# A recurrent (HGRN2) layer: the low parts of the projection weights are formed by VectorE in place of GpSimd

## The chip, the cores and the metric

One core of a Trainium2 chip. The metric is the device time of one execution in microseconds (us), the median of several runs.

## The reference

A backbone of two layers over 1024 latent tokens and 256 context tokens, width 1024: a bidirectional gated linear recurrence (HGRN2), then multi-head latent attention (MLA). Each layer normalises its input, scales and shifts it by vectors made from a conditioning vector (adaLN), mixes the tokens, projects back and adds a gated, normalised residual. The change lies in the first layer. What it computes, cut to its core:

```python
q, i_in, f_fw, f_bw, z = jnp.split(h @ w_in, 5, axis=-1)     # 16 heads of 128 each
for d, g in enumerate((f_fw, f_bw)):
    f = lb[d] + (1 - lb[d]) * sigmoid(g);  k = (1 - lb[d]) * sigmoid(-g)
# per head and direction, v = i_in, q = silu(q):
S_t = diag(f_t) S_{t-1} + k_t v_t^T;   o_t = S_t^T q_t
o = o_forward + o_backward
y = (rmsnorm(o, gain) * silu(z)) @ w_out
```

All of it is in float32. The kernel keeps that precision in the projections by writing each factor as a rounded high part and the rest, the low part, and adding three products.

## The kernel before, in words

**Matrices in two parts.** `split` makes the parts: ScalarE casts the source to the rounded type (line 214, `hi`), then an engine subtracts (line 215, `lo = src - hi`); without `eng` that engine is VectorE. `load_split` loads a piece of 128x1024 float32 (512 KB) into a `raw` tile by a DMA from SyncE's queue (line 286) and splits it into `wh` and `wl`. `wpool` has four buffers each for `wh` and `wl` and two for `raw`; the small adaLN products of line 125, which VectorE makes beside the recurrence, use the `raw` buffers too. `mm3` multiplies: three matmuls (lines 263 to 265), high by high, high by low, low by high.

**The layer.** `hgrn` runs over 16 heads. The 10 token tiles of 128 tokens (two of context, eight of latent) stand in groups of four, four and two. For a head it takes three weight tiles (`load_qfb`: q and the two forget gates), and for every group multiplies them (`feed`, PSUM tiles `g`), makes the gates and the keys (`gates`), and then in `levels` the products within a tile, in seven levels of a binary tree. A level has one product on TensorE (`products`, line 335, PSUM tiles `lv`, two banks, which are shared with `g`), whose result is put into `A` by VectorE (line 351, `copy_predicated`) or ScalarE, and VectorE and ScalarE make the operands `KX` and `QX` of the next level from those of this one (lines 384 to 386, 398). So a level's product waits for VectorE's work of the level before, and TensorE is given projection products of the next group, of the values or of the gate `z` in between. On every even head `values` projects the values of two heads (two weight tiles). Then come the projection of `z` (one weight tile, lines 540 to 548), the states between tiles (`states`, and `recur`, line 446), and the readout, whose rsqrt runs on GpSimd (lines 80 and 81).

**The order.** Nothing here is ordered by hand: a scheduler orders every engine's instructions by its own estimate of when each can start. Each engine then runs its list in that order, so an instruction that waits holds up all that stand behind it on its engine. GpSimd's list in this layer holds the subtractions of `wl` and the rsqrt work, and nothing else.

**The names.** `wl` and `wh` are the parts of a weight tile, `lv` a level product, `KX` and `QX` its operands, `QY` and `K` the other halves that are kept for later levels, `A` the products that are put together, `Ta` and `Tb` the decays of a level, `kd` and `q` the operands of the diagonal.

Of the kernel before, what the change touches and what calls it, by code (L numbers as in the profile page):

```python
# [18 lines left out]
P = 128  # L19
# [21 lines left out]
class Net:  # L41
# [12 lines left out]
    def t(self, pool, shape, dt, tag, **kw):  # L54
        self.uid += 1
        return pool.tile(shape, dt, tag=tag, name=f"{tag}_{self.uid}", **kw)
# [425 lines left out]

    def load_qfb(self, wpool, h):
        return [
            self.load_split(wpool, self.a["w_qfbz"][h, :, m], [P, self.KT, P], "w", eng=self.nc.gpsimd)
            for m in range(3)
        ]

# [5 lines left out]
    def values(self, pool, wpool, pp, hh, hl, h):  # L494
        nc, t, KT = self.nc, self.t, self.KT
        w = min(2, self.NH - h)
        kh = max(1, KT // 2)
        wv = [
            self.load_split(wpool, self.a["w_v"][h // 2, :, k : k + kh, : w * P], [P, kh, w * P], "w", eng=nc.gpsimd)
            for k in range(0, KT, kh)  # L500
        ]
        V2 = t(pool, [P, self.NT, 2, P], F32, "V")
        for c in range(0, self.NT, 2):
            m = min(2, self.NT - c)
            ps = t(pp, [P, 2, 2, P], F32, "g")
            for j in range(m):
                sl = slice((c + j) * P, (c + j + 1) * P)
                for k in range(KT):
                    wh, wl = (x[:, k % kh] for x in wv[k // kh])
                    self.mm3(ps[:, j, :w], hh[:, k, sl], hl[:, k, sl], wh, wl, k == 0, k == KT - 1)  # L510
            nc.scalar.copy(V2[:, c : c + m, :w], ps[:, :m, :w])
        return V2

    def hgrn(self, pool, wpool, pp, hh, hl, yT, wq0, ps0, side, late):
        nc, t, KT, a = self.nc, self.t, self.KT, self.a
        for h in range(self.NH):
            wq = wq0 if h == 0 else self.load_qfb(wpool, h)
            sts = []
            for c0, n in self.groups:
                G = n * P  # L520
                sl = slice(c0 * P, c0 * P + G)
                st = {}
                for m in range(3):
                    if h == 0 and ps0 and m < len(ps0[0]):
                        ps = ps0[0][m]
                    else:
                        ps = t(pp, [P, 512], F32, "g")[:, :G]
                        for k in range(KT):
                            self.feed([ps], wq[m : m + 1], (c0, n), hh, hl, k)
                    self.gates(h, m, ps, G, st, pool)  # L530
                if h == 0 and (c0, n) == self.groups[min(1, len(self.groups) - 1)]:
                    late()
                if h == 0 and ps0:
                    ps0.pop(0)
                self.levels(pool, pp, st, G)
                sts.append(st)
            if h % 2 == 0:
                V2 = self.values(pool, wpool, pp, hh, hl, h)
            V = V2[:, :, h % 2]
            wz = self.load_split(wpool, a["w_qfbz"][h, :, 3], [P, KT, P], "w", eng=nc.gpsimd)  # L540
            Z = t(pool, [P, self.NT * P], F32, "Z")
            for c0, n in self.groups:
                sl = slice(c0 * P, (c0 + n) * P)
                ps = t(pp, [P, 512], F32, "g")[:, : n * P]
                for k in range(KT):
                    self.feed([ps], [wz], (c0, n), hh, hl, k)
                nc.scalar.activation(Z[:, sl], ps, AF.Sigmoid)
                nc.vector.tensor_tensor(Z[:, sl], Z[:, sl], ps, ALU.mult)
            US = t(pool, [P, 2, self.NT, P], F32, "US")
            for g, st in zip(self.groups, sts):  # L550
                self.states(pool, pp, st, g, V, US)
            prev = self.recur(sts, US)
            for g, st in zip(self.groups, sts):
                self.readout(h, pool, pp, st, g, V, Z, US, prev, yT)
            side(h)
# [811 lines left out]
```

## Time and profile before

| | |
|---|---|
| median of 3 runs | 3215.31 us (3214.12 to 3218.83) |
| the profiled execution, its own time | 3215.2 us |
| its span, first to last instruction | 3213.4 us |
| mean granted TensorE clock | 0.995 of full speed |
| busy: TensorE, VectorE, ScalarE, GpSimd | 3155.7, 2092.5, 1685.5, 437.1 us |

The recurrent layer goes from about 70 to 1670 us of the span; the output projection, MLA and its output projection follow. Busy shares are means over stages with different limits; what a change in one stage is worth is read from that stage's stretch, from what TensorE waits for there.

### The profile page before, as it was taken

To read this page: it belongs to the slowest core of one execution; us is meant where nothing else is said; L and a number is where in the kernel's file an instruction comes from. 1 tells how busy PE (TensorE), PEld (TensorE's weight loads), DVE (VectorE), ACT (ScalarE), POOL (GpSimd) and SP (SyncE) were. 2 spreads that over 40 slices of the span, in tenths; PEclk is the share of its full clock that TensorE was granted. 3 is DMA by queue.
4 is the path that set the end of the run, shared out by engine and by line. 5 is a ranking of instruction groups with operands and counts; after the bars stand their busy time and mean duration, and the time that the engine had idled before them with its cause. 6 is when DMAs were issued, how large, how long until landed. Compare 5 with 4: busy or idle time off the path is not lost.

```text
span 3213.4 us, 52381 instructions
## 1 busy us (share of the span) xinstructions
PE 3155.7 (98%) x19860; PEld 2827.5 (88%) x19860; DVE 2092.5 (65%) x4680; ACT 1685.5 (52%) x4215; POOL 437.1 (14%) x424
## 2 busy tenths in 40 slices
PE   8899999999999999999999999999999999999999
PEld 7888989889898898898998878888999999999887
DVE  7676577666774767737566464535777777777742
ACT  6455455554554545545455565314666666666532
POOL 2111111111111121111100212210000000000000
PEclk8999999999999999999999999999999999999999
DMA  5110211102111120100115662331100010101261
GB/s 209 40 55 22 73 35 48 55 29 79 36 42 55 35 73 29 35 29 27 36 35 172 233 227 86 115 125 53 39 32 30 27 37 29 37 21 37 75 214 59
DMA packets 100012, 218.94 MB, mean 68 GB/s; under 512 B 10288, under 2 KB 47408, under 8 KB 99760
## 3 DMA queue, kind: packets, MB, share of 16 engines
q1 hardware_dynamic: 99760, 215.59, 20.3%
q8 instruction: 157, 2.57, 0.3%
q14 instruction: 95, 0.78, 0.1%
HBM read 175.70 MB, written 39.85 MB: 67 GB/s over the span
## 4 chain that ended last, share of the span: by engine, by line
PE 80%; DVE 11%; issue 4%; ACT 2%; DMA 2%; POOL 1%; SPq 0%; DVEq 0%; POOLq 0%; ACTq 0%
PE g L264 9%; PE g L265 9%; PE g L263 9%; PE lv L335 6%; PE pt L878 4%; PE o L464 3%; PE s L831 2%; PE pv L263 2%; PE pv L264 2%; PE pv L265 2%; PE s L832 2%; PE s L834 2%; PE s L835 2%; PE s L833 2%; PE lv L263 2%
## 5 line engine op out<-in xcount | busy, mean ns | idle before, releaser
L263 PE MATMUL g<-hh,wh 128*128 128x512 f32 (+1 forms) x1512 | 547.5, 362 | 0.3 <-DVE hh L253 0.2
L264 PE MATMUL g<-hh,wl 128*128 128x512 f32 (+1 forms) x1512 | 544.9, 360 | 0.0
L265 PE MATMUL g<-hl,wh 128*128 128x512 f32 (+1 forms) x1512 | 544.6, 361 | 0.0
L263 PEld LDWEIGHTS g<-hh,wh 128*128 128x128 f32 x1512 | 286.9, 190 | 37.1 <-DVE hh L253 0.4
L264 PEld LDWEIGHTS g<-hh,wl 128*128 128x128 f32 x1512 | 286.9, 190 | 35.4
L265 PEld LDWEIGHTS g<-hl,wh 128*128 128x128 f32 x1512 | 286.0, 189 | 35.4
L215 POOL TENSOR_TENSOR wl<-raw,wh 128x1024 fp32r<-128x1024 f32 x77 | 195.3, 2541 | 872.0 <-ACT wh L214 864.4
L335 PE MATMUL lv<-QX,KX 128*128 128x128 f32 x1920 | 268.5, 278 | 28.5 <-DVE KX L384 12.9
L837 DVE TENSOR_REDUCE mx<-s 128x1 f32<-128x512 f32 (+1 forms) x384 | 229.6, 598 | 96.1 <-PE s L835 95.1
L847 ACT ACTIVATE pr<-s,nm 128x512 f32<-128x512 f32 (+1 forms) x384 | 232.7, 614 | 101.4 <-DVE nm L843 95.1
L335 PEld LDWEIGHTS lv<-QX,KX 128*128 128x128 f32 x1920 | 245.8, 192 | 44.2 <-issue 16.4
L214 ACT CAST wh<-raw 128x1024 fp32r<-128x1024 f32 (+1 forms) x170 | 178.2, 1052 | 131.4 <-PE lv L264 38.9
L214 ACT CAST ph<-pt 128x512 fp32r<-128x512 f32 x320 | 187.7, 587 | 95.0 <-PE pt L878 85.3
L215 DVE TENSOR_TENSOR pl<-pt,ph 128x512 fp32r<-128x512 f32 x320 | 219.2, 686 | 12.5 <-ACT ph L214 12.4
L385 ACT COPY KX<-K 128x256 f32<-128x256 f32 (+1 forms) x288 | 109.2, 379 | 171.3 <-DVE K L386 127.5
L263 PE MATMUL g<-wh,hh 128*128 128x256 f32 (+2 forms) x676 | 197.4, 293 | 0.0
L263 PE MATMUL pv<-ph,vh 128*128 128x256 f32 x640 | 196.6, 307 | 0.0
L265 PE MATMUL g<-wl,hh 128*128 128x256 f32 (+2 forms) x676 | 196.3, 291 | 0.0
L878 PE MATMUL pt<-ident,pr 128*128 128x128 f32 x1280 | 191.8, 272 | 0.1
L264 PE MATMUL g<-wh,hl 128*128 128x256 f32 (+1 forms) x654 | 188.6, 288 | 0.0
L215 DVE TENSOR_TENSOR wl<-raw,wh 128x1024 fp32r<-128x1024 f32 x93 | 117.0, 1263 | 106.5 <-ACT wh L214 105.6
L265 PE MATMUL pv<-pl,vh 128*128 128x256 f32 x640 | 180.0, 281 | 0.0
(552 smaller groups left out, 8129.0 us busy)
## 6 DMA issues: line engine op xcount, KB each, us to landing
raw<-in_w_o SPq DMA_DIRECT2D x64, 512.0 KB, 3.9
raw<-in_w_qfbz SPq DMA_DIRECT2D x61, 512.0 KB, 3.8
raw<-in_ada_wT SPq DMA_DIRECT2D x32, 512.0 KB, 3.5
raw<-in_w_mo SPq DMA_DIRECT2D x24, 512.0 KB, 3.7
raw<-in_w_v SPq DMA_DIRECT2D x16, 512.0 KB, 3.6
yT<-Z SPq DMA_DIRECT2D x32, 256.0 KB, 2.0
raw<-in_w_z SPq DMA_DIRECT2D x16, 512.0 KB, 3.9
pyr<-yT SPq DMA_DIRECT2D x64, 128.0 KB, 3.7
```

The lines of the kernel that those rows point to most:

```text
L214: nc.scalar.copy(hi, src)
L215: (eng or nc.vector).tensor_tensor(lo, src, v32(hi), ALU.subtract)
L263: mm(ps, lh, rh, start=first, stop=False)
L264: mm(ps, ll, rh, start=False, stop=False)
L265: mm(ps, lh, rl, start=False, stop=last)
L335: nc.tensor.matmul(ps[:, sl], lhs[:, sl], rhs[:, sl], start=True, stop=True)
L385: cp(m12(N[:]), m12(Y))
L464: nc.tensor.matmul(o[:, sl], l, r, start=i == 0, stop=i == len(ops) - 1)
L831: mm(s[:, :w], qah[:, js], st["kh"][:, ks], start=True, stop=False)
L837: nc.vector.tensor_reduce(mx[:, b : b + 1], s[:, :w], AX.X, ALU.min)
L847: nc.scalar.activation(pr[:, o : o + w], sc[b][:, :w], AF.Exp, bias=nm, scale=-1.0, accum_out=sm[:, b : b + 1],)
L878: nc.tensor.transpose(tp[:, c, j * P : (j + 1) * P], prs[i][:, k * P : (k + 1) * P], self.ident)
```

## The change

All weight tiles of `hgrn` but the first three, which are loaded at the start by another function, had GpSimd as the engine of the subtraction. The change leaves the argument out, so that VectorE does it. There are 77 such tiles: three for each of 15 heads, 16 of `values` and 16 of `z`. Shapes, buffers, DMAs and casts stay.

```diff
     def load_qfb(self, wpool, h):
         return [
-            self.load_split(wpool, self.a["w_qfbz"][h, :, m], [P, self.KT, P], "w", eng=self.nc.gpsimd)
+            self.load_split(wpool, self.a["w_qfbz"][h, :, m], [P, self.KT, P], "w")
             for m in range(3)
         ]
...
         wv = [
-            self.load_split(wpool, self.a["w_v"][h // 2, :, k : k + kh, : w * P], [P, kh, w * P], "w", eng=nc.gpsimd)
+            self.load_split(wpool, self.a["w_v"][h // 2, :, k : k + kh, : w * P], [P, kh, w * P], "w")
             for k in range(0, KT, kh)
         ]
...
-            wz = self.load_split(wpool, a["w_qfbz"][h, :, 3], [P, KT, P], "w", eng=nc.gpsimd)
+            wz = self.load_split(wpool, a["w_qfbz"][h, :, 3], [P, KT, P], "w")
```

The scheduler sees another program and orders the layer anew. Three places of head 6, in its second group of four tiles, show how. There `lv_7321`, `lv_7337`, `lv_7353` and `lv_7369` are four level products in turn, `wl_7643` is the second tile of the values' weights and `wl_7900` that of `z`.

VectorE before, from the second level's `KX` to the two writes of `A`:

```order
L384 TENSOR_TENSOR KX_7343<-KX_7327,Ta_7335 128x64x2x2
L398 TENSOR_TENSOR Tb_7351<-Ta_7335 128x256
L297 TENSOR_TENSOR q_7461<-q_7461,g_7436 128x256
L384 TENSOR_TENSOR QX_7344<-QX_7328,Ta_7335 128x64x2x2
L386 TENSOR_TENSOR K_7248<-K_7248,T_1323_7247 128x128x2
L386 TENSOR_TENSOR QY_1326_7250<-QX_7328,Ta_7335 128x64x4
L384 TENSOR_TENSOR QX_7360<-QX_7344,Tb_7351 128x32x2x4
L386 TENSOR_TENSOR K_7248<-KX_7327,Ta_7335 128x64x4
L386 TENSOR_TENSOR QY_1326_7250<-QX_7344,Tb_7351 128x32x8
L398 TENSOR_TENSOR Ta_7367<-Tb_7351 128x128
L351 COPY_PREDICATED A_1330_7314<-mask_62,lv_7321 128x512
L351 COPY_PREDICATED A_1330_7314<-mask_62,lv_7337 128x512
```

And now:

```order
L384 TENSOR_TENSOR KX_7343<-KX_7327,Ta_7335 128x64x2x2
L398 TENSOR_TENSOR Tb_7351<-Ta_7335 128x256
L215 TENSOR_TENSOR wl_7643<-raw_7645,wh_7644 128x1024
L386 TENSOR_TENSOR QY_1326_7250<-QX_7249,T_1323_7247 128x128x2
L384 TENSOR_TENSOR QX_7344<-QX_7328,Ta_7335 128x64x2x2
L386 TENSOR_TENSOR K_7248<-K_7248,T_1323_7247 128x128x2
L351 COPY_PREDICATED A_1330_7314<-mask_62,lv_7321 128x512
L215 TENSOR_TENSOR wl_7900<-raw_7902,wh_7901 128x1024
L386 TENSOR_TENSOR QY_1326_7250<-QX_7328,Ta_7335 128x64x4
L384 TENSOR_TENSOR QX_7360<-QX_7344,Tb_7351 128x32x2x4
L386 TENSOR_TENSOR K_7248<-KX_7327,Ta_7335 128x64x4
L351 COPY_PREDICATED A_1330_7314<-mask_62,lv_7337 128x512
```

The two subtractions stand in VectorE's list now. The first `A` has moved ahead of five operations, from the `QY` of 128x64x4 to `Ta_7367`; the last two of these stand behind the second `A`, and `KX_7359` follows them.

TensorE before, between two level products (`g_7498` is a projection of the forget gate, `g_7650` one of the values):

```order
L335 MATMUL lv_7353<-QX_7344,KX_7343 128x128 x4
L265 MATMUL g_7498<-hl_127,wh_6997 128x256
L263 MATMUL g_7498<-hh_126,wh_6997 128x256
L264 MATMUL g_7498<-hh_126,wl_6996 128x256
...
L263 MATMUL g_7650<-wh_7638,hh_126 128x256
L264 MATMUL g_7650<-wh_7638,hl_127 128x256
L265 MATMUL g_7650<-wl_7637,hh_126 128x256
L335 MATMUL lv_7369<-QX_7360,KX_7359 128x128 x4
```

And now:

```order
L335 MATMUL lv_7353<-QX_7344,KX_7343 128x128 x4
L265 MATMUL g_7498<-hl_127,wh_6997 128x256
L263 MATMUL g_7650<-wh_7638,hh_126 128x256
L264 MATMUL g_7650<-wh_7638,hl_127 128x256
L265 MATMUL g_7650<-wl_7637,hh_126 128x256
...
L263 MATMUL g_7650<-wh_7644,hh_126 128x256
L264 MATMUL g_7650<-wh_7644,hl_127 128x256
L265 MATMUL g_7650<-wl_7643,hh_126 128x256
...
L335 MATMUL lv_7369<-QX_7360,KX_7359 128x128 x4
```

Between the two level products stood 10 projection matmuls and now stand 32; six of the `g_7498` moved ahead of `lv_7353`.

ScalarE before, up to the cast of the `z` weights:

```order
L341 COPY A_1330_7314<-lv_7315 128x512
L385 COPY KX_7343<-K_7248 128x64x4
L385 COPY QX_7360<-QY_1326_7250 128x32x8
L306 ACTIVATE T_1361_7464<-g_7468 128x256
L310 ACTIVATE K_1362_7465<-g_7468 128x128x2
L214 CAST wh_7901<-raw_7902 128x1024
```

And now, with what follows it:

```order
L341 COPY A_1330_7314<-lv_7315 128x512
L214 CAST wh_7901<-raw_7902 128x1024
L425 COPY ev_8003<-tp_8002 128x256
...
L385 COPY KX_7343<-K_7248 128x64x4
L306 ACTIVATE T_1361_7464<-g_7468 128x256
L310 ACTIVATE K_1362_7465<-g_7468 128x128x2
```

The cast moved ahead of four operations, of which the first two wait for VectorE.

## Rows read from the trace of the kernel before

**Rows 1.** Stretches: span, busy us of PE, PEld, DVE, ACT, POOL, clock, DMA share, GB/s

```profile
78.00:200.00 122.00, 111.15 (x768) 102.54 (x769) 76.06 (x186) 58.93 (x150) 21.83 (x15) 0.97 0.15 46
200.00:1650.00 1450.00, 1426.55 (x9652) 1305.31 (x9651) 954.65 (x2355) 745.88 (x1984) 227.11 (x154) 1.00 0.14 43
```

**Rows 2.** TensorE's groups, 78 to 1650 us: busy us, mean ns | idle before, releasers

```profile
L335 PE MATMUL lv<-QX,KX 128*128 128x128 f32 x1800 | 252.3, 278 | 28.5 <-DVE KX L384 12.9 <-DVE A L351 9.0 <-DVE Tb L398 3.4
```

**Rows 3.** TensorE's waits, 78 to 200 and 200 to 1650 us: total, times, longest

```profile
PE tp L236 <- DVE US L229: 4.0, 1, 4.0
...
PE lv L335 <- DVE KX L384: 10.8, 19, 1.9
PE lv L335 <- DVE A L351: 9.0, 13, 0.9
```

**Rows 4.** GpSimd's groups, 78 to 1650 us: the subtraction

```profile
L215 POOL TENSOR_TENSOR wl<-raw,wh 128x1024 fp32r<-128x1024 f32 x77 | 195.3, 2541 | 872.0 <-ACT wh L214 864.4 <-DMA raw<-in_w_v 7.6
```

**Rows 5.** VectorE's groups by shape, 78 to 1650 us

```profile
L125 DVE SCALAR_TENSOR_TENSOR raw<-raw,silu 128x1024 f32<-128x1024 f32 x56 | 68.0, 1215 | 22.8 <-DMA raw<-in_ada_wT 22.5
L384 DVE TENSOR_TENSOR KX<-KX,Tb 128x256 f32<-128x256 f32 x60 | 64.6, 1076 | 0.0
L384 DVE TENSOR_TENSOR QX<-QX,Ta 128x256 f32<-128x256 f32 x91 | 52.7, 579 | 0.0
L386 DVE TENSOR_TENSOR QY<-QX,Ta 128x256 f32<-128x256 f32 x90 | 50.3, 559 | 0.0
...
L384 DVE TENSOR_TENSOR QX<-QX,Tb 128x256 f32<-128x256 f32 x60 | 24.9, 415 | 0.0
L384 DVE TENSOR_TENSOR KX<-KX,Tb 128x128 f32<-128x128 f32 x30 | 23.0, 767 | 0.0
...
L384 DVE TENSOR_TENSOR QX<-QX,Tb 128x128 f32<-128x128 f32 x30 | 8.4, 281 | 0.0
```

**Rows 6.** VectorE in order of time, head 6: start us, us, what

```profile
725.41 2.27 DVE L384 TENSOR_TENSOR QX<-QX,Ta 128x256 f32<-128x256 f32 x1
...
728.15 0.42 DVE L386 TENSOR_TENSOR QY<-QX,Ta 128x256 f32<-128x256 f32 x1
...
729.70 1.57 DVE L351 COPY_PREDICATED A<-mask,lv 128x512 f32<-128x512 uint8 x2
731.16 2.26 DVE L384 TENSOR_TENSOR KX<-KX,Tb 128x256 f32<-128x256 f32 x1
```

**Rows 7.** GpSimd in order of time, the same stretch

```profile
724.21 3.18 POOL L215 TENSOR_TENSOR wl<-raw,wh 128x1024 fp32r<-128x1024 f32 x1 [19.34 <-ACT wh L214]
730.75 2.38 POOL L215 TENSOR_TENSOR wl<-raw,wh 128x1024 fp32r<-128x1024 f32 x1 [3.36 <-ACT wh L214]
```

**Rows 8.** TensorE in order of time, the same stretch; in brackets idle time and releaser

```profile
725.98 0.37 PE L265 MATMUL g<-hl,wh 128*128 128x256 f32 x1
...
729.30 0.28 PE L263 MATMUL g<-hh,wh 128*128 128x256 f32 x1
729.42 0.28 PE L264 MATMUL g<-hh,wl 128*128 128x256 f32 x1
730.57 1.13 PE L335 MATMUL lv<-QX,KX 128*128 128x128 f32 x8 [0.87 <-DVE A L351]
...
733.56 0.68 PE L335 MATMUL lv<-QX,KX 128*128 128x128 f32 x4 [0.68 <-DVE KX L384]
```

**Rows 9.** The line of the subtraction, VectorE's share, whole span: ns min/median/max

```profile
L215 DVE TENSOR_TENSOR wl<-raw,wh x93: 1204/1225/2104, 1674.7 to 3051.8; 128x1024 fp32r<-128x1024 f32 x92, 128x896 fp32r<-128x896 f32 x1
```

**Rows 10.** ScalarE in order of time, head 6: the cast of the z weights

```profile
729.61 1.07 ACT L214 CAST wh<-raw 128x1024 fp32r<-128x1024 f32 x1
```

**Rows 11.** ScalarE in order of time, the cast of head 7's query weights

```profile
754.20 1.05 ACT L214 CAST wh<-raw 128x1024 fp32r<-128x1024 f32 x1 [0.95 <-DMA raw<-in_w_qfbz]
```

**Rows 12.** DMA issues by line: size of one, median us to landing

```profile
raw<-in_w_qfbz SPq DMA_DIRECT2D x61, 512.0 KB, 3.8
```

**Rows 13.** VectorE's waits, 1650 us to the end: total, times, longest

```profile
DVE wl L215 <- ACT wh L214: 105.6, 57, 8.6
```

## The prediction, made before the changed kernel ran

> **What bounds the kernel now.** I read the stretches first. From 200 to 1650 us, which is the recurrent layer without its start, TensorE is busy for 1426.55 of 1450 us, so 23.45 us are idle; from 78 to 200 us, the start, 111.15 of 122 us, so 10.85 us are idle [rows 1]. The clock is at full speed in the first and 0.97 in the second, so nothing is to be won there. The layer is bound by TensorE, and 34.3 us, the sum of the two, is the most that a change on another engine can give back: TensorE's own work stays the same. Behind 1650 us the order of every engine that computes is the same in the changed program, so nothing is costed there.
>
> Next I asked who makes TensorE wait. Nearly all of the idle time stands before one group, the level products of line 335: 28.5 us [rows 2]. In the long stretch it is released by VectorE, 10.8 us by `KX` (line 384), the next level's operand, and 9.0 us by `A` (line 351), which empties the PSUM bank that the next product needs; at the start one wait of 4.0 us is for VectorE's scaling on line 229 [rows 3]. So VectorE is late at some places, though it is busy only 954.65 of the 1450 us [rows 1].
>
> Then I asked why it is late. GpSimd's 77 subtractions take 2541 ns each [rows 4]. The same VectorE instruction has very different means according to where it falls [rows 5]: the 128x256 product is 415 ns as `QX<-QX,Tb` and 1076 as `KX<-KX,Tb`; the 128x128 one 281 and 767. In time it is plain: in head 6 GpSimd starts at 724.21 and runs for 3.18 us, and the VectorE product that begins at 725.41 takes 2.27 us and ends with it, within 0.3 us; GpSimd starts again at 730.75, and the product of 731.16 takes 2.26 us [rows 6, 7]. TensorE then idles 0.87 us (until 730.57, for the `A` that stood behind the first) and 0.68 us (until 733.56, for the second itself) [rows 8]. VectorE reads two SBUF tensors in each of these, and GpSimd's subtraction reads two also; one stands still until the other is done, at some 1.85 us (2.27 less 0.42) a time. The Trainium skill, "SBUF — State Buffer", section "Who interferes with whom", says just that: a VectorE instruction with two SBUF inputs and a GpSimd instruction that reads SBUF exclude each other, and the later one blocks fully. By that rule the stalls go when GpSimd's subtractions go, as I forecast below.
>
> **The change, term by term.**
> *Removed from VectorE: the blocked time.* Four groups of rows 5 give it: 60 x (1076 - 415) = 39.7 us, 30 x (767 - 281) = 14.6, 91 x (579 - 415) = 14.9, 90 x (559 - 415) = 13.0, together 82 us. Some smaller groups are blocked too, so that this is a lower bound; 77 x 1.85 = 142 us is the upper. Between them I take 77 x 0.8 x 1.85 = 114 us: about one subtraction in five falls where VectorE has nothing to do.
> *Added to VectorE:* 77 subtractions. The same line already runs there later in the kernel, with a median of 1225 ns [rows 9]: 94 us. VectorE's busy time thus stays about where it is: +12 us at the lower bound, -20 us by my figure.
> *Moved:* the scheduler wrote the orders of TensorE, VectorE and ScalarE anew for the layer; GpSimd only loses rows, and the DMA queue's order is the same. That is where the time is decided, so I worked through head 6. In the changed order five operations (from the `QY` at 728.15 to the start of `A` at 729.70, 1.55 us) fall behind `A`, and one subtraction is put ahead of it. `A` then starts at 729.70 - 1.85 - 1.55 + 1.23 = 727.5 and is done at 728.3, where it was done at 730.4. TensorE reaches `lv_7353` later than before: it was there at 729.70 (730.57 less 0.87) and now has six more projection products ahead of it, which start 0.12 us apart [rows 8], so 730.4. No wait is left, with 2 us to spare. Behind `A` stand the second subtraction (1.23), three of the five operations (1.0), the other `A` (0.74), an adaLN product (1215 ns, rows 5) and two short ones (0.6): `KX_7359` begins at about 733.1 and is ready at 733.5, as before. But TensorE has 32 projection products ahead of `lv_7369` in place of 10, so it comes there at 730.4 + 0.9 + 32 x 0.12 = 735.1. The 0.68 us go too. The orders of the odd heads show the same shape, and the other pairs of heads repeat this one.
> *The casts.* VectorE takes over GpSimd's wait for ScalarE's cast, and behind a waiting subtraction stands the level chain. In head 6 the first cast was done by 724.21, when GpSimd began [rows 7], and VectorE comes at about 725.2, the place where its blocked product stood [rows 6]. The second starts at 729.61 [rows 10], which would be late; but in the changed order it stands four rows earlier on ScalarE, so that it waits only for the last use of the weights whose buffer it takes. TensorE left them at 726.35 (725.98 and 0.37, rows 8), so it is done at about 727.4, before VectorE comes at 728.3. The query weights of odd heads are closest: there the cast waited for the DMA until 754.20 [rows 11]. Its DMA starts when an adaLN product frees a `raw` buffer and lands 3.8 us later [rows 12]; with the cast (1.05) that is 4.9 us. In the changed order 16 VectorE operations stand between that adaLN product and the subtraction, an estimate of 5.2 us by their pitch in the trace. So I cost the wait at nothing there, and at up to 2.7 us should VectorE come as early as in the trace. About three subtractions per pair of heads stand ahead of `Z`, where VectorE has no other work; their waits cost nothing.
> *The start.* Four subtractions fall from 78 to 123 us, where VectorE itself is the limit. I take half of the 10.85 us as won, 5.4 us; nothing would be the lower end and all of it the upper.
> *GpSimd* keeps its short rsqrt work. Nothing waits for more than that.
>
> The sum: I take four fifths of the 23.45 us, 18.8, since a few new waits will come up in an order that no run has shown, and 5.4 at the start: 24 us. From the profiled execution's own 3215.2 us that gives 3191 us. It stands 0.1 us from the median of the runs, so I carry the figure over. The ends of this case alone: 32 us won (3183), if nearly all idle time goes, and 12 us (3203), if half of the long stretch and nothing at the start does.
>
> **The rivals.**
> *VectorE waits for the casts, and gives the gain back.* The wait that was GpSimd's, where nobody stood behind it, is then VectorE's. Later in the kernel VectorE waits 105.6 us at 57 of the 93 such subtractions, up to 8.6 us [rows 13], 1.85 us each. For it: the casts that wait for DMA or for a buffer. Against: in those later stages VectorE had little else to do, and in the changed order TensorE has more work between the level products. If a dozen of the query weights' subtractions wait 2 us, 24 us are given back: 3215 us.
> *Slower: the same wait, at every subtraction in the level chain.* Some 54 of the 77 stand there. If half of them wait 1.85 us, that is 50 us against 34.3 to be won at the very most: 3215.2 + 16 = 3231 us. It decides once the waits in the chain that TensorE feels pass 34 us. Head 6 worked out speaks against it.
> *Slower, by load: the long products have another cause.* Then 94 us are added to VectorE and none is taken away. TensorE now idles 34.3 us for some 114 us of lateness, 0.3 us for each; 94 x 0.3 = 28 us: 3243 us. Rows 6 and 7 speak against it. The Trainium skill, "Perfetto Trace Analysis", section "Optimizing Scalar/DVE Operations", advises moving work off a saturated VectorE, to GpSimd among others, which taken alone speaks against this change, though it adds that between those two a move might not help. The trace agrees with the addition: 114 us of blocking is more than the 94 us of the work.
> *The change does little:* TensorE's idle time only moves to other places, 3215 us. It is counted with the first rival.
>
> **How the numbers follow.** The forecast, the blocking goes and the new order covers the rest, gets 0.75; given back to within 6 us gets 0.15; slower 0.10 (0.07 by the casts, 0.03 by load). The range is 3181 to 3213 us: it holds the first case and its bounds with some 2 us beyond them, and the better part of the second; what is left out is the slower cases and the rest of the second, about 2 in 10. A difference of 0.2%, 6.4 us, is about what a measurement of this kernel can tell from none; so faster 0.75, same 0.15, slower 0.10.
>
> **What would show it.** Right: in the layer no VectorE product of 128x256 stays near 2.2 us, `KX<-KX,Tb` has a mean near 0.42 us, the 77 subtractions on VectorE take about 1.23 us, VectorE's busy time from 200 to 1650 us changes by less than 25 us, and TensorE's idle time there is near 5 us. Wrong in the cast step: VectorE's idle time ahead of `wl` for `wh` is over 20 us in places with a level product behind it. Wrong in the cause: the products stay long without GpSimd beside them. Wrong in the order: TensorE waits for line 335 as long as before, behind other releasers.

## The result and the profile after

The changed kernel takes 3175.76 us (median of four runs, 3174.58 to 3176.91); the kernel before, measured beside it, 3215.44 us. The ratio is 0.9875, 95% interval 0.9858 to 0.9892: faster by 39.7 us. The forecast was 24 us, and its range reached 34 us. The sign and the cause were right, the size was not.

The stretches of the changed kernel, with the columns of [rows 1]:

```profile
78.00:200.00 122.00, 114.64 (x800) 105.53 (x800) 79.75 (x206) 61.29 (x158) 4.49 (x8) 0.99 0.16 51
200.00:1650.00 1450.00, 1450.00 (x9888) 1335.54 (x9887) 962.17 (x2498) 771.27 (x2034) 49.80 (x84) 1.00 0.14 44
```

From 200 to 1650 us TensorE shows no idle time at all, where it had 23.45 us. The 77 subtractions have left GpSimd (227.11 us there before, 49.80 now), yet VectorE, which took them, is busy only 7.5 us longer, and that in a stretch that holds 2% more of the matmuls (9888 against 9652). For the same work, from the last product of line 464 (the readout) of head 0 to that of head 15, its busy time fell from 1028.2 to 1006.1 us.

VectorE's groups by shape, 78 to 1650 us, answer to [rows 5] and, in the first line, to [rows 9]:

```profile
L215 DVE TENSOR_TENSOR wl<-raw,wh 128x1024 fp32r<-128x1024 f32 x80 | 97.5, 1219 | 74.8 <-ACT wh L214 74.8
...
L384 DVE TENSOR_TENSOR QX<-QX,Ta 128x256 f32<-128x256 f32 x96 | 40.1, 418 | 0.0
L386 DVE TENSOR_TENSOR QY<-QX,Ta 128x256 f32<-128x256 f32 x96 | 40.0, 417 | 0.0
...
L384 DVE TENSOR_TENSOR KX<-KX,Tb 128x256 f32<-128x256 f32 x64 | 26.4, 412 | 0.0
...
L384 DVE TENSOR_TENSOR KX<-KX,Tb 128x128 f32<-128x128 f32 x30 | 8.5, 283 | 0.0
```

TensorE's group of [rows 2], the same stretch:

```profile
L335 PE MATMUL lv<-QX,KX 128*128 128x128 f32 x1888 | 260.0, 276 | 1.6 <-DVE QX L384 0.9 <-DVE KX L384 0.6
```

Each of these groups has one duration now: `KX<-KX,Tb` went from 1076 to 412 ns, `QX<-QX,Ta` from 579 to 418. The idle time before the level products fell from 28.5 to 1.6 us.

Head 6 at the place of [rows 6 to 8], some 16 us earlier in the span. VectorE in order of time:

```profile
709.84 1.21 DVE L215 TENSOR_TENSOR wl<-raw,wh 128x1024 fp32r<-128x1024 f32 x1
710.98 0.63 DVE L386 TENSOR_TENSOR QY<-QX,T 128x256 f32<-128x256 f32 x1
711.53 0.41 DVE L384 TENSOR_TENSOR QX<-QX,Ta 128x256 f32<-128x256 f32 x1
...
712.42 0.73 DVE L351 COPY_PREDICATED A<-mask,lv 128x512 f32<-128x512 uint8 x1
713.05 1.20 DVE L215 TENSOR_TENSOR wl<-raw,wh 128x1024 fp32r<-128x1024 f32 x1
...
717.54 0.41 DVE L384 TENSOR_TENSOR KX<-KX,Tb 128x256 f32<-128x256 f32 x1
```

TensorE, the two level products that stalled before:

```profile
714.81 0.28 PE L263 MATMUL g<-hh,wh 128*128 128x256 f32 x1
714.93 0.28 PE L264 MATMUL g<-hh,wl 128*128 128x256 f32 x1
715.05 1.06 PE L335 MATMUL lv<-QX,KX 128*128 128x128 f32 x8
...
719.66 0.28 PE L263 MATMUL g<-wh,hh 128*128 128x256 f32 x1
719.78 1.06 PE L335 MATMUL lv<-QX,KX 128*128 128x128 f32 x8
```

`A` is written at 713.15 and TensorE comes to the product that needs its bank at 715.05, 1.9 us later; `KX` is ready at 717.95 and TensorE comes at 719.78. The two bracketed waits of [rows 8] are gone, with some 1.9 us to spare each. These margins are what the experiments below eat up.

The casts of the same two tiles on ScalarE, in order of time:

```profile
706.84 1.07 ACT L214 CAST wh<-raw 128x1024 fp32r<-128x1024 f32 x1
710.62 1.05 ACT L214 CAST wh<-raw 128x1024 fp32r<-128x1024 f32 x1 [0.85 <-PE g L265]
```

VectorE's wait for casts, 78 to 1650 us (total, times, longest):

```profile
DVE wl L215 <- ACT wh L214: 74.8, 30, 12.6
```

In head 6 both casts end before VectorE comes. Elsewhere it does wait, 74.8 us in 30 places, but TensorE shows no idle time for it: from 78 to 1650 us it idles 1.6 us before the level products in all.

### The profile page after: what moved, and what is told of

Same layout as the page of the kernel before. It is cut to its first block, busy times and chain, and to the rows that moved or that the text cites. A ratio compares the mean times of both kernels' runs of the same rounds, so it can differ in the third digit from the quotient of the medians.

```text
span 3174.2 us, 52378 instructions
## 1 busy us (share of the span) xinstructions
PE 3142.8 (99%) x19860; PEld 2822.7 (89%) x19860; DVE 2069.2 (65%) x4757; ACT 1687.8 (53%) x4215; POOL 239.4 (8%) x347
## 5 line engine op out<-in xcount | busy, mean ns | idle before, releaser
L215 DVE TENSOR_TENSOR wl<-raw,wh 128x1024 fp32r<-128x1024 f32 (+1 forms) x170 | 210.0, 1238 | 181.9 <-ACT wh L214 181.8
L351 DVE COPY_PREDICATED A<-mask,lv 128x512 f32<-128x512 uint8 (+1 forms) x240 | 153.2, 638 | 51.1 <-PE lv L335 50.6
```

The lines of the kernel that those rows point to most:

```text
L215: (eng or nc.vector).tensor_tensor(lo, src, v32(hi), ALU.subtract)
L351: self.nc.vector.copy_predicated(A, self.mask[:, lev].unsqueeze(1).broadcast_to(list(A.shape)), p3)
```

## The experiments

My theory: VectorE's products of two SBUF tensors stand still beside GpSimd's subtraction, and TensorE lost its time by that. The rivals: the new order alone brought the gain; GpSimd was merely late with `wl`; or each microsecond of VectorE costs TensorE 0.3. "Blocked" below is a VectorE instruction from 78 to 1650 us that is over 0.3 us longer than the short ones (20th percentile) of its line and shape; its excess is added up.

### GpSimd's work put back beside the new order

```diff
-            self.split(hi[:, sl], lo[:, sl], raw, eng=eng)
+            self.split(hi[:, sl], lo[:, sl], raw, eng=eng); extra and nc.gpsimd.tensor_tensor(self.t(self.wpool, list(raw.shape), F32, "pj"), v32(hi[:, sl]), v32(hi[:, sl]), ALU.subtract)
```

`extra` is set at the three calls that the change touches.

> The changed kernel, and behind each of the 77 splits GpSimd subtracts two SBUF tensors of the same size into a tile that nobody reads. The orders of TensorE, VectorE, ScalarE and the DMA queue are those of the changed kernel, row for row; only GpSimd's work is back. Theory (VectorE's two-input products stand still beside GpSimd's subtraction, and that was the loss): products of 128x256 near 2.2 us are back, and the time is between 3195 and 3235 us, since VectorE now has the blocking and the 94 us of subtractions too. Rival (the new order alone brought the gain, the blocking was covered): the long products come back and the time stays at 3174 to 3179 us. Rival (GpSimd was only late with wl): no long products, 3174 to 3179 us.

Measured: 3206.78 us (ratio to before 0.9974, 0.9962 to 0.9986), 31.0 us above the changed kernel. Its stretch from 200 to 1650 us:

```profile
200.00:1650.00 1450.00, 1430.83 (x9689) 1310.80 (x9688) 1027.31 (x2434) 751.63 (x1990) 238.11 (x154) 1.00 0.14 44
```

GpSimd's group, 78 to 1650 us:

```profile
L287 POOL TENSOR_TENSOR pj<-wh 128x1024 f32<-128x1024 f32 x77 | 206.6, 2683 | 866.1 <-ACT wh L214 865.4
```

The place of head 6 lies 11.6 us later in this span; GpSimd there, in order of time:

```profile
719.60 1.92 POOL L287 TENSOR_TENSOR pj<-wh 128x1024 f32<-128x1024 f32 x1 [20.24 <-ACT wh L214]
723.42 2.65 POOL L287 TENSOR_TENSOR pj<-wh 128x1024 f32<-128x1024 f32 x1 [1.90 <-ACT wh L214]
```

VectorE in order of time:

```profile
719.68 2.50 DVE L325 SCALAR_TENSOR_TENSOR kd<-K,lbs,kd 128x512 f32<-128x512 f32 x1
...
724.23 2.34 DVE L386 TENSOR_TENSOR QY<-QX,T 128x256 f32<-128x256 f32 x1
...
727.37 0.72 DVE L351 COPY_PREDICATED A<-mask,lv 128x512 f32<-128x512 uint8 x1
```

TensorE in order of time:

```profile
726.80 0.28 PE L264 MATMUL g<-hh,wl 128*128 128x256 f32 x1
728.24 1.13 PE L335 MATMUL lv<-QX,KX 128*128 128x128 f32 x8 [1.15 <-ACT T L306]
```

The two VectorE instructions take 1.64 and 1.71 us more than in the changed kernel (0.86 and 0.63) and end 0.66 and 0.50 us behind GpSimd's. `A` comes 3.33 us late (727.37 - 11.62 - 712.42); the margin of 1.9 us is used up, and the rest is TensorE's: it would have gone on at 726.92 and does at 728.24, 1.32 us lost. (`A` is done at 728.09. The `T` that the bracket names is done 0.1 us later; it stands on ScalarE behind a copy that waited for VectorE's `K`, so that it is late by the same cause.) In all, 68 instructions are blocked by 1.56 us each. With the orders of TensorE, VectorE and ScalarE unchanged, GpSimd's presence alone costs 31 of the 39.7 us, as the theory had it. The rivals that gave the whole gain to the order or to `wl`'s lateness fall: the order is the new one here, and nobody reads what GpSimd writes.

### One input, half, three quarters

The same with a copy, and then with the subtraction over a part of the columns (here half; three quarters likewise; each line is shown from `extra` on):

```diff
-extra and nc.gpsimd.tensor_tensor(self.t(self.wpool, list(raw.shape), F32, "pj"), v32(hi[:, sl]), v32(hi[:, sl]), ALU.subtract)
+extra and nc.gpsimd.tensor_copy(self.t(self.wpool, list(raw.shape), F32, "pj"), v32(hi[:, sl]))
...
+extra and nc.gpsimd.tensor_tensor(self.t(self.wpool, [P, raw.shape[1] // 2] + shape[2:], F32, "pj"), v32(hi[:, : raw.shape[1] // 2]), v32(hi[:, : raw.shape[1] // 2]), ALU.subtract)
```

> As the run before, but GpSimd copies one SBUF tensor of 128x1024 into the tile that nobody reads; the orders of the other engines are again those of the changed kernel. If any GpSimd instruction that reads SBUF blocks VectorE's two-input ones, products stand still for the copy's length, and the time lies above 3180 us, in proportion to that length against the subtraction's 2.5 us. If the two inputs on GpSimd's side are needed, no product of 128x256 is longer than 0.5 us and the time stays at 3174 to 3179 us.

> As the run with GpSimd's unread subtraction, but with half of its columns (128x512); the orders of the other engines are those of the changed kernel, row for row. Blocked VectorE instructions should be about 0.9 us longer than alone, between the copy's 0.67 and the full subtraction's 1.56. If TensorE loses in proportion to what VectorE is blocked: 31 x 0.9 / 1.56 = 18 us, 3194 us. If the order covers a delay up to a certain length and only the rest is lost (the copy's cost nothing; 68 x (1.56 - s) = 31 gives s = 1.1 us): 3175 to 3181 us.

> As the run with half of GpSimd's unread subtraction, now with three quarters of its columns; the orders of the other engines are those of the changed kernel, row for row. The blocking should lie between 0.67 and 1.56 us, at about 1.1. If a delay of up to some length is covered and only what is longer is lost: at most 3182 us by s = 1.1 us. If TensorE's loss grows evenly from 0.67 us on: half of the full subtraction's 31 us, 3191 us.

Measured: 3175.73 us (ratio to before 0.9874, 0.9858 to 0.9891), 3175.52 us (0.9874, 0.9857 to 0.9890) and 3187.99 us (0.9910, 0.9894 to 0.9927). GpSimd's group, 78 to 1650 us, of the copy:

```profile
L287 POOL COPY pj<-wh 128x1024 f32<-128x1024 f32 x77 | 139.4, 1811 | 889.5 <-ACT wh L214 889.0
```

Of half the subtraction:

```profile
L287 POOL TENSOR_TENSOR pj<-wh 128x512 f32<-128x512 f32 x77 | 141.7, 1840 | 887.2 <-ACT wh L214 886.5
```

Of three quarters:

```profile
L287 POOL TENSOR_TENSOR pj<-wh 128x768 f32<-128x768 f32 x77 | 169.6, 2203 | 878.2 <-ACT wh L214 877.6
```

The copy does block, though it reads one tensor: 61 VectorE instructions by 0.67 us each, 41 us in all. TensorE loses none of it: my expectation, that any blocking would show in the time, missed. Half a subtraction blocks as much (60 by 0.68 us, not the 0.9 that I expected) and costs nothing either. Three quarters block 68 by 1.10 us and cost 12.2 us: above the 3182 that a sharp limit at 1.1 us allowed, near the 3191 of an even growth. The limit lies lower. A line through this run and the first, 68 x k x (1.10 - s) = 12.2 and 68 x k x (1.56 - s) = 31.0, gives k = 0.6 and s = 0.8 us: of a blocking, the first 0.8 us are covered on the mean, and 0.6 of the rest reaches TensorE. Two unknowns from two runs fit exactly whatever the law is; the test is another run. For the kernel before, which is not in the fit (60 blocked by 1.90 us each, 113.7 us in all), that makes 60 x 0.6 x 1.1 = 40 us; 39.7 were measured, though in another order, whose margins need not be the same.

### A short blocking in the order before

```diff
-        (eng or nc.vector).tensor_tensor(lo, src, v32(hi), ALU.subtract)
+        eng.tensor_copy(lo, v32(hi)) if eng else nc.vector.tensor_tensor(lo, src, v32(hi), ALU.subtract)
```

> The kernel before, but GpSimd copies the high part into wl in place of subtracting (the low parts of the 77 weight tiles are thus wrong; all later work is the same). TensorE's order is that of before but for 441 of 16264 places, VectorE does not get the 94 us, and the blocked time should be 0.67 us an instruction, as beside the copy in the changed kernel, where it cost nothing. If the lock is nearly the whole of it and before's order covers 0.67 us too: 3175 to 3181 us. If the new order is worth some 10 us by itself, since before's has less work between the level products: 3184 to 3192 us. Over 3200 us would mean that the length of the blocking is not what costs.

Measured: 3178.84 us (0.9882, 0.9867 to 0.9897). Its stretch:

```profile
200.00:1650.00 1450.00, 1449.67 (x9888) 1335.58 (x9887) 914.27 (x2426) 769.74 (x2031) 136.51 (x154) 1.00 0.14 44
```

GpSimd's group, 78 to 1650 us:

```profile
L215 POOL CAST wl<-wh 128x1024 fp32r<-128x1024 f32 x77 | 95.7, 1243 | 917.8 <-ACT wh L214 899.0 <-PE lv L335 18.9
```

59 instructions are blocked by 0.57 us each, and 37 of the 40 us are won, with nearly the order of before and without VectorE's 94 us. So the order and the move of the work are worth some 3 us, which the intervals of the two ratios do not tell from nothing; the length of the blocking is what cost.

### Cutting the subtraction instead of moving it

The kernel before, with four GpSimd instructions a tile:

```diff
-        (eng or nc.vector).tensor_tensor(lo, src, v32(hi), ALU.subtract)
+        [(eng or nc.vector).tensor_tensor(lo[:, i : i + j], src[:, i : i + j], v32(hi[:, i : i + j]), ALU.subtract) for j in [src.shape[1] // 4 if eng else src.shape[1]] for i in range(0, src.shape[1], j)]
```

> The kernel before, with GpSimd's subtraction cut into four of a quarter of the columns each; TensorE's and ScalarE's orders are those of before, row for row, and VectorE does not get the 94 us. If the length of one blocking decides (VectorE comes in between two pieces, 0.6 us each, and a delay that short is covered): 3175 to 3190 us, near the changed kernel without moving the work. If the sum of the blocking decides, or VectorE does not get in between the pieces: 3210 to 3220 us.

Measured: 3197.55 us (0.9943, 0.9928 to 0.9958), between the two kernels and outside of both expectations: 18 of the 40 us are won. Its stretch:

```profile
200.00:1650.00 1450.00, 1435.59 (x9738) 1318.22 (x9737) 946.72 (x2385) 753.25 (x1998) 279.49 (x364) 1.00 0.14 43
```

GpSimd's group, 78 to 1650 us:

```profile
L215 POOL TENSOR_TENSOR wl<-raw,wh 128x256 fp32r<-128x256 f32 x308 | 258.0, 870 | 800.2 <-ACT wh L214 800.2
```

VectorE does come in between the pieces, and a blocking is only 0.52 us, but there are 166 of them, about two for one tile (86 us / 77 = 1.1 us a tile). My reading is that these add up before the next level product, as one of 1.1 us would; the runs don't separate that from the longer total on GpSimd.

### More work for VectorE

```diff
-            self.split(hi[:, sl], lo[:, sl], raw, eng=eng)
+            self.split(hi[:, sl], lo[:, sl], raw, eng=eng); extra and nc.vector.tensor_tensor(lo[:, sl], raw, v32(hi[:, sl]), ALU.subtract)
```

> The changed kernel, with each of the 77 subtractions done twice by VectorE, the second time with the same result: 77 x 1.22 = 94 us more on VectorE, no GpSimd work. Theory (TensorE does not wait for VectorE any more, and the order leaves slack): 3176 to 3184 us. Rival (each us of VectorE costs 0.3 us of TensorE, as worked out from the kernel before): 3176 + 28 = 3204 us.

Measured: 3187.56 us (0.9911, 0.9896 to 0.9925), 11.8 us above the changed kernel: outside of both expectations. At 11.8 / 94 = 0.13 us for each us of VectorE it is far below the load theory's price. Its stretch:

```profile
200.00:1650.00 1450.00, 1445.92 (x9821) 1327.11 (x9820) 1025.26 (x2542) 766.95 (x2017) 65.70 (x84) 1.00 0.14 43
```

GpSimd has no work of its own added, and yet is busy 65.70 us where the changed kernel has 49.80. Its rsqrt, 78 to 1650 us, a mean of 1100 ns in the changed kernel:

```profile
L81 POOL TENSOR_TENSOR rsq_m<-rsq_m,nhalf 128x4 f32<-128x4 f32 x30 | 48.6, 1621 | 2.5
```

One place of the readout, GpSimd, ScalarE and TensorE in order of time:

```profile
276.32 3.63 POOL L81 TENSOR_TENSOR rsq_m<-rsq_m,nhalf 128x4 f32<-128x4 f32 x1
279.99 1.14 ACT L475 ACTIVATE ev<-o,rsq_m 128x128 f32<-128x128 f32 x4 [2.42 <-POOL rsq_m L81]
282.25 1.10 PE L478 MATMUL tp<-ident,ev 128*128 128x128 f32 x4 [0.29 <-ACT ev L475]
```

Seven of these rsqrt instructions take 3.6 us in place of 1.0 (the longest in the changed kernel is 1.27), each while VectorE runs two-input products one behind the other, from 276.10 to 279.08 us here. ScalarE's scaling waits for the rsqrt, and TensorE's transposes of line 478 for that. Counted from start to start, as the next section explains, these transposes lose 8.3 us more than in the changed kernel, and the level products 2.1, of 10.4 us lost in the layer. So most of the loss is the same blocking the other way round, VectorE holding GpSimd where the two now fall side by side; it is not the level products waiting for a busier VectorE.

### A part of the change at a time

Two runs. In the first the argument stays for the values and z, in the second for q, f and b; as changes to the changed kernel:

```diff
-            self.load_split(wpool, self.a["w_v"][h // 2, :, k : k + kh, : w * P], [P, kh, w * P], "w")
+            self.load_split(wpool, self.a["w_v"][h // 2, :, k : k + kh, : w * P], [P, kh, w * P], "w", eng=nc.gpsimd)
...
-            wz = self.load_split(wpool, a["w_qfbz"][h, :, 3], [P, KT, P], "w")
+            wz = self.load_split(wpool, a["w_qfbz"][h, :, 3], [P, KT, P], "w", eng=nc.gpsimd)
```

```diff
-            self.load_split(wpool, self.a["w_qfbz"][h, :, m], [P, self.KT, P], "w")
+            self.load_split(wpool, self.a["w_qfbz"][h, :, m], [P, self.KT, P], "w", eng=self.nc.gpsimd)
```

> Only the 45 subtractions of the q, f and b weights are on VectorE; the 32 of the values and of z stay on GpSimd. If each GpSimd subtraction costs the same: 45/77 of the gain of 39.7 us is kept, 3192 us. If the loss came from the blocking in the level chains of the even heads, where the values' weights are split: 3200 us or more. If the q, f and b weights were the cause: near 3178 us. Mean of the 128x256 products between 0.42 and the 0.56 to 1.08 us of the kernel before.

> Only the 32 subtractions of the values and of z are on VectorE; the 45 of q, f and b stay on GpSimd. The run with q, f and b alone on VectorE kept 22.0 us. If the stalls add up, this one keeps the rest of the whole change's 40 us, 18 us: 3195 to 3202 us. If it is the new order that brings the gain, the parts don't add up: below 3190 or above 3207 us.

Measured: 3194.66 us (0.9933, 0.9918 to 0.9947) and 3189.02 us (0.9916, 0.9902 to 0.9931): 22.0 and 27.0 us kept, 49 together where the whole change has 40. The first is near its equal share, the second missed its band and lies in the one (below 3190) that stood for a gain by the new order. The runs above speak against that reading. The parts overlap: the values and z left on GpSimd block 32 instructions by 54 us, q, f and b 29 by 51, so that the blocking adds up (105 against 113.7 us), but the loss does not (18.9 + 13.3 against 39.7). That fits margins which two stalls in one pair of heads must share; but each of the two kernels also has an order of its own, I did not show it, and it stays open.

## Why the prediction was right or wrong

**Right: the cause.** 60 of the 77 subtractions blocked VectorE, by 113.7 us; 114 were forecast. The share of 0.8 in that sum, for which the prediction shows no row, came to 0.78. None is blocked in the changed kernel. The subtractions take 1219 ns. VectorE's busy time rose by 7.5 us in the fixed stretch, which holds more work now; for the same work it fell by 22 us, near the -20 of the text.

**Right: head 6.** The margins were worked out as 2 us and 1.6 us and came to 1.9 and 1.83. The casts' waits exist, 74.8 us, and cost TensorE nothing, as said. The rivals of waiting, of load and of "little" are all refuted by the time and by TensorE's busy 1450.00 of 1450 us.

**Right by luck: the start.** The last product of line 464 for head 0 starts at 197.55 us before and at 192.62 after: 4.9 us, forecast 5.4. But the half was taken between nothing and all without a row that speaks for it, so that its closeness is luck.

**Wrong: the layer, 18.8 us, and the bound above it.** From that mark to the same product of head 15 (1744.93 before, 1705.84 after) the distance shrank by 34.2 us. (That last readout runs beside the output projection, behind the 1670 us at which the layer was said to end; TensorE idles for 1.5 us of the time from 1650 us to it.) The step that failed is the sentence that "34.3 us, the sum of the two, is the most that a change on another engine can give back": 39.7 were given back. Two errors lie in the term. The smaller one, some 4 us, is the fifth that was held back for new waits: none came, and nearly all of the idle time went, 23.2 us between the marks. The larger one, 11 us, is that idle time was taken for lost time. A row's idle time counts from the end of the matmul before, and that end lies behind the next start when nothing waits: a 128x256 matmul is shown as 0.28 us long, yet its successor starts 0.12 us after it, in the rows of head 6 above as in [rows 8]. So at 730.57 TensorE lost 730.57 - 729.42 - 0.12 = 1.03 us where the row says 0.87, and a stall behind such a matmul hides 0.16 us; one of less than that shows no idle time at all. The prediction itself used the 0.12 us to count matmuls, and did not use it there.

That this holds for the whole layer can be seen in every run that lost time (the copy, half the subtraction and the short blocking in the order before lost less than 0.4 us). Distance between the two marks over that of the changed kernel (1513.2 us), beside the idle time between the marks over the changed kernel's (1.8 us):

| kernel | lost, us | idle shown, us |
|---|---|---|
| before | 34.2 | 23.2 |
| GpSimd's work put back | 27.3 | 18.3 |
| quarters on GpSimd | 19.5 | 13.9 |
| q, f, b alone | 15.4 | 11.1 |
| values and z alone | 13.3 | 7.1 |
| three quarters put back | 11.5 | 6.8 |
| twice on VectorE | 10.4 | 3.8 |

The loss is 1.4 to 1.9 times the idle time shown, and 2.7 times in the last run. Counted by starts instead (each matmul's distance from the start before it, less the median of both kernels for its pair of shapes, where over 0.06 us), 200 to 1650 us gives 67.2 us before and 34.3 after, in 485 and 406 places: 32.9 us of difference, nearly the 34.2 measured. The level products account for it: 36.2 us stand before line 335 in the kernel before and 1.2 in the changed one. The remaining places are each shorter than 0.1 us, nearly all before projection products, and there without any blocking; what they are, the runs don't say.

The range had its lower end at the bound and fell with it. The trace of the kernel before, counted by starts, would have given the 36.2 us as the most to be won there; with 5.4 for the start that is 41.6 us, and 39.7 lies below it.

## What to carry to other kernels

When an instruction has two lengths in one program, look at what the engines beside it were doing at that moment: taking the other engine's work away can gain more than the work costs where it goes. What such a blocking cost here was, in the main, its length less the margin that the order gives the next dependent product; shortening it below that (some 0.8 us on the mean) was as good as removing it. The runs that showed this have GpSimd copy in place of subtracting, or subtract over half of the columns; the one way tried that keeps the whole work on GpSimd, four pieces, won 18 of the 40 us. Look at both directions, too: the engine that takes the work over can in turn hold up what the other still does, as in the run with the subtraction done twice. And take a TensorE stall from start to start, not from the idle time shown: that is a lower bound on the loss, so it must not be used as an upper bound on a gain.

## What the runs showed of the hardware

A GpSimd copy, with one SBUF input, blocks VectorE's two-input instructions as a subtraction of the same duration does: not held up, both take 1.04 us (10th percentile), and the blocked instruction is longer by 0.67 and 0.68 us. The blocking follows GpSimd's own length at a distance of 0.3 to 0.5 us: 1.04, 1.47, 1.89 and 2.38 us (10th percentile of its instruction in each run) go with a mean of 0.67, 1.10, 1.56 and 1.90 us. The rule of the Trainium skill, "SBUF — State Buffer", section "Who interferes with whom", says that a VectorE instruction with two SBUF inputs contends with a GpSimd instruction that reads SBUF, and sets no number of inputs for the latter. The trace agrees: the copy held 61 instructions. What I had not expected is that 41 us of blocking in so short pieces cost nothing in the time.

It is also mutual, and here the later one is held. With GpSimd's work put back, its instruction of 719.60 takes 1.92 us and holds VectorE's `kd` of 719.68, while that of 723.42 starts during VectorE's subtraction (723.10 to 724.32) and takes 2.65 us itself. With the subtraction done twice, VectorE's run of six two-input products (276.10 to 279.08) holds an rsqrt of GpSimd over tensors of 128x4 for 2.6 us.
